# Rotation of q and k on VectorE or GpSimd by plan, bias rows on the sync queue, and a longer DMA latency in the plan

## The chip, the core and the metric

The kernel runs on one core of a Trainium2 chip. A core has five engines that run their own instruction streams in order and wait for one another through semaphores: TensorE (PE, matmuls; PEld is its weight load), VectorE (DVE), ScalarE (ACT), GpSimd (POOL) and SyncE (SP, which here only issues DMA transfers). The metric is device time in microseconds (us) of one execution. The kernel before takes 1269.06 us, the median of three runs (1265.8 to 1271.94).

## The reference

Four decoder layers on x of 256 tokens by 1024, float32. Layers 0 and 3 mix tokens with attention A (a sliding window of 128, 16 query heads on 4 key heads, biases and a learned sink for each head), layer 1 with B (three dilated attentions, merged by their softmax denominators), layer 2 with C (here causal attention in a single block). A mixer is: project to q, k, v; rotate the first 16 of the 64 columns of each head of q and k; attend; project back. After it come a layer norm of alpha\*x + mixer(x), a SwiGLU network of width 2816 and a second layer norm.

```python
def apply_rope(x, cos, sin):
    half = ROT_DIM // 2                       # ROT_DIM = 16, heads of 64
    x1, x2 = x[..., :half], x[..., half:ROT_DIM]
    return concat([x1 * c - x2 * s, x2 * c + x1 * s, x[..., ROT_DIM:]])

def mixer_a(x, w_qkv, b_qkv, sinks, w_o, b_o, cos, sin):
    qkv = x @ w_qkv + b_qkv
    q, k, v = apply_rope(q part), apply_rope(k part), v part
    o, _ = block_attention(q, k, v, 128, 127, True, sinks)
    return o @ w_o + b_o

for i in range(4):
    x = layer_norm(alpha * x + mixer[i % 3](x))
    x = layer_norm(alpha * x + swiglu(x))
```

## The kernel before, in words

**Numbers.** Weights and activations are float32 and are multiplied as two float16 parts each: `whi`, `wlo` of a weight (scaled by 256), `xth`, `xtl` of the transposed input. One product is three matmuls into one PSUM bank (`mm3`, L293 to L295).

**Weights.** They come in chunks of 1024 x 512 (for the last projection of the network also 768 x 512), each chunk in pieces of 128 x 1024. A piece is loaded by a DMA on SP into one of four buffers `raw` (L250), ScalarE makes `whi` of it (L229), VectorE makes `wlo` (L221), and the buffer is then free for the next load. Up to five chunks are alive. The four pieces of the first chunk do not use `raw`: they are loaded at the start, between the four halves of x, into buffers that are not needed yet (L91; their names are htl, oth, otl).

**The plan.** The program of PE, ACT, DVE and POOL is written out in the order that a small planner in the kernel finds while it is built. It keeps a clock `T` for each engine. `do(engine, us, dep, fn)` gives an instruction out if its input is there by the plan, or files it under its due time `dep`; `spend` moves PE's clock on by each matmul and gives out what has become due. A piece of weights is fed when both ACT and DVE would be idle; its first split is due at `T["DMA"] + 2.0`, where `T["DMA"]` is the time at which its buffer came free plus 1.45 (L253 to L257). What the planner believes decides the order alone; at run time each engine goes through its stream in that order and waits where an input is late. SP is not among the engines of the plan: its DMAs stand in an order of their own, given below.

**q and k.** When a chunk of q and k columns has been summed (8 steps over k, for each half t of the tokens), ACT copies the bank to an SBUF tile `qkv` (L864 in mixer A, L924 in B and C), `rope` rotates it in place with four instructions on GpSimd (L408 to L411; the plan gives them 2.2 us), and PE turns it by transposes (L304), after which ACT and DVE split the result (`qkh`, `qkl`). There are 44 such rotations: 12 in the two mixers A (4 of them of half width), 24 in B, 8 in C.

**The start.** `first_chunk` lays out the first chunk of mixer A: dummy matmuls (L1013), transposes of x as its halves land, the first steps over k for both t; then `bias_parts` makes the two float16 parts of mixer A's bias (L1023 on ACT, L1024 on DVE) and copies them to two rows of the tile `abias` by two DMAs that POOL issues (L1020); `angles` and `tables` make the sines and cosines. The bias enters each bank by a matmul with a tile of ones (L300), after the fifth step over k. The raw bias, `araw`, is loaded by the last of four DMAs on POOL (L95).

Of the kernel before, what the change touches and what calls it, by code (L numbers as in the profile page):

```python
# [18 lines left out]
P = 128  # L19
# [24 lines left out]
def trunk(ctx, tc, a, out):  # L44
    nc = tc.nc
    ctx.enter_context(tc.manual_schedule(engines={getattr(mybir.EngineType, e) for e in ("PE", "Activation", "DVE", "Pool")}))
    pool = lambda name, bufs, **kw: ctx.enter_context(tc.tile_pool(name=name, bufs=bufs, **kw))
    RING, RAWS = 5, 4
    const = pool("const", 1)
    raw_p = pool("raw", RAWS)  # L50
    w_p = pool("w", RING)
# [24 lines left out]
    araw = const.tile([P, 2, 20], F32, name="araw")  # L76
# [7 lines left out]
    big0 = big.tile([P, NFB, SEQ], F16, name="htl").rearrange("p f s -> p (f s)").bitcast(F32)  # L84
    stage = [big0[:, :1024], big0[:, 1024:2048]] + [
        big.tile([P, NK, SEQ], F16, name=n).rearrange("p f s -> p (f s)").bitcast(F32) for n in ("oth", "otl")]
    for h in range(2):
        for t in range(NT):
            nc.sync.dma_start(X[t][:, h * 512:h * 512 + 512], a["x"][t * P:(t + 1) * P, h * 512:h * 512 + 512])
            i = 2 * h + t  # L90
            nc.sync.dma_start(stage[i], a["w_a"][0, 0][:, 1024 * i:1024 * i + 1024])  # L91
    nc.gpsimd.dma_start(pos_i, a["positions"].rearrange("(t p) -> p t", p=P))
    nc.gpsimd.dma_start(inv, a["inv"].partition_broadcast(P))
    nc.gpsimd.dma_start(sinks, a["a_sinks"].partition_broadcast(P))
    nc.gpsimd.dma_start(araw, a["a_bias"].rearrange("j (p c) -> p j c", p=P))  # L95

# [5 lines left out]
    T = {"PE": 0.0, "ACT": 0.0, "DVE": 0.0, "POOL": 0.0, "DMA": 0.0}  # L104
# [5 lines left out]
    def do(e, us, dep, fn, then=None, key=None):  # L110

        def give():
            fn()
            T[e] = max(T[e], dep) + us
            if then is not None:
                then(T[e] + HOP)
        if dep <= max(T["PE"], T[e]):
            give()
        else:
            serial[0] += 1  # L120
            due.append((dep, serial[0], give, key))
            due.sort(key=lambda d: d[:2])
# [86 lines left out]
    def new_w(src, n):  # L209
        ring["alive"] += 1  # L210
        assert ring["alive"] <= RING
        hi, lo = (w_p.tile([P, 4096], F16, name=nm) for nm in ("whi", "wlo"))
        return {"hi": hi, "lo": lo, "src": src, "n": n, "ready": [None] * (n // 2), "raw": None, "next": 0,
                "parts": tuple(p.rearrange("p (k n) -> p k n", n=512) for p in (hi, lo))}

    def piece(c, i, r, there, last=None):
        s = slice(1024 * i, 1024 * i + 1024)
        ring["flying"] += 1

        def low(end):  # L220
            do("DVE", dve(1024), end, lambda: nc.vector.scalar_tensor_tensor(  # L221
                c["lo"][:, s], r, WS, c["hi"][:, s], op0=OP.mult, op1=OP.subtract), landed, "w")

        def landed(end):
            c["ready"][i] = end
            ring["flying"] -= 1
            if last is not None:
                last(end)
        do("ACT", act(1024), there, lambda: nc.scalar.activation(c["hi"][:, s], r, AF.Copy, scale=WS), low, "w")  # L229

    def feed_one():

        c = ring["now"]
        if c is None:
            if ring["alive"] == RING:
                return False
            src = next(weights, None)
            if src is None:
                return False
            c = ring["now"] = new_w(*src)  # L240
            loaded.append(c)
        i = c["next"]
        c["next"] += 1
        until(lambda: raws[0] < NEVER)
        T["DMA"] = max(T["DMA"], raws.pop(0)) + 1.45
        raws.append(NEVER)
        slot[0] += 1
        number = slot[0]
        r = raw_p.tile([P, 1024], F32, name="raw")
        nc.sync.dma_start(r, c["src"][:, 1024 * i:1024 * i + 1024])  # L250

        def last(end):

            raws[RAWS - 1 - (slot[0] - number)] = end
        if c["next"] == len(c["ready"]):
            ring["now"] = None
        piece(c, i, r, T["DMA"] + 2.0, last)  # L257
        return True

    slot = [0]  # L260
# [138 lines left out]
    def rope(y, n, t, nh, dep, then):  # L399

        def turn():
            t1 = two.tile([P, 8, ROT], F32, name="rope1")[:, :nh]
            t2 = two.tile([P, 8, ROT], F32, name="rope2")[:, :nh]
            cb = cc[:, t:t + 1, :].to_broadcast([P, nh, ROT])
            sb0 = ss[:, t:t + 1, :h8].to_broadcast([P, nh, h8])
            sb1 = ss[:, t:t + 1, h8:].to_broadcast([P, nh, h8])
            e = nc.gpsimd
            e.tensor_tensor(t1, y[:, :, :ROT], cb, op=OP.mult)  # L408
            e.tensor_tensor(t2[:, :, :h8], y[:, :, h8:ROT], sb0, op=OP.mult)  # L409
            e.tensor_tensor(t2[:, :, h8:], y[:, :, :h8], sb1, op=OP.mult)  # L410
            e.tensor_tensor(y[:, :, :ROT], t1, t2, op=OP.add)  # L411
        do("POOL", 2.2, dep, turn, then)

    def transposed(y, t, n, dst, key):

# [15 lines left out]
    turn = [0]  # L431
# [578 lines left out]
    def spin(n):  # L1010
        ps, b = bank()
        for _ in range(n):
            nc.tensor.matmul(ps, idle[:, :P], idle, start=True, stop=True)  # L1013
        T["PE"] += 0.43 * n
        b["free"] = T["PE"]

    def bias_rows(j, queue):

        for i in range(2):
            queue.dma_start(abias[i:i + 1].rearrange("o (p c) -> o p c", p=P), aparts[:, i, j])  # L1020

    def bias_parts():
        nc.scalar.activation(aparts[:, 0], araw, AF.Copy, scale=WS)  # L1023
        nc.vector.scalar_tensor_tensor(aparts[:, 1], araw, WS, aparts[:, 0], op0=OP.mult, op1=OP.subtract)  # L1024
        bias_rows(0, nc.gpsimd)

    def first_chunk(XT, evac):

        c = new_w(*next(weights))
        c["next"] = 4  # L1030
        land = [3.6, 5.2, 6.0, 7.6, 8.4, 10.0, 10.8, 12.4]
        spin(6)
        wait(land[0])
        transpose_x(0, XT, 0)
        piece(c, 0, stage[0], land[1])
        spin(3)
        wait(land[2])
        transpose_x(1, XT, 0)
        piece(c, 1, stage[1], land[3])
        spin(1)  # L1040
        p = [proj(XT, c, t, evac) for t in range(NT)]
        for f in p[0][:2] + p[1][:2]:
            f()
        T["DMA"] = 12.4
        for t in range(NT):
            wait(land[4 + 2 * t])
            transpose_x(t, XT, 1)
        for f in p[0][2:4] + p[1][2:4]:
            f()
        for i in (2, 3):  # L1050
            piece(c, i, stage[i], land[1 + 2 * i])
        until(lambda: c["ready"][3] is not None)
        bias_parts()
        do("DVE", 2.2, 0.0, angles)
        T["ACT"] += 2.0
        ring["on"] = True
        for f in p[0][4:6] + p[1][4:6]:
            f()
        do("DVE", 1.0, T["ACT"], tables)
        for f in p[0][6:] + p[1][6:]:  # L1060
            f()
        done()
# [3 lines left out]
    for li in range(DEPTH):  # L1066
        kind, j = li % 3, li // 3
# [94 lines left out]
```

## Time and profile before

| | before |
|---|---|
| median of 3 runs | 1269.06 us (1265.8 to 1271.94) |
| the profiled execution | 1272.32 us, of which the span from the first to the last instruction is 1270.5 us |
| busy in the span: PE, DVE, ACT, POOL | 1240.2, 878.8, 668.9, 131.1 us |
| mean granted TensorE clock | 0.993 of 2.4 GHz |

The span is what the trace shows; the 1.8 us around it are the same execution's time outside. The ends of matmuls are modelled, so that PE looks busy between two matmuls that follow each other closely; a wait of PE shows as a start that comes late, with the idle time before it in brackets and the engine or DMA that ended it. Line numbers of this section and of the rows are those of the kernel before; in the changed kernel they are one to two higher.

### The profile page before, as it was taken

The numbers are of one execution on the slowest core, as the hardware profiler recorded it, in microseconds if no ns is written. First come the engines' busy times: TensorE is split into PE (matmuls) and PEld (weight loads), VectorE is DVE, ScalarE is ACT, GpSimd is POOL, SyncE is SP. The second block draws the span as 40 slices with busy tenths as digits, with TensorE's granted clock in tenths as the row PEclk, the third lists the DMA queues.
The fourth block names the chain that finished last, engine by engine and source line by source line (L and its number), as shares of the span: only waits on it lengthen the run. The fifth ranks groups of instructions, "written<-read, shape, count | busy, mean of one in ns | idle before, by whom it ended". The sixth has DMA issues, their size and how long they took to land.

```text
span 1270.5 us, 24604 instructions
## 1 busy us (share of the span) xinstructions
PE 1240.2 (98%) x9990; PEld 828.2 (65%) x9990; DVE 878.8 (69%) x1415; ACT 668.9 (53%) x1102; POOL 131.1 (10%) x270
## 2 busy tenths in 40 slices
PE   7999999999999999999999999999999999999997
PEld 3558888444555555588884445588884455888843
DVE  4798876556676676778665677778665578886632
ACT  4775664336666656546543367546543276465410
POOL 3310000013021203000000122000000132000000
PEclk9999999999999999999999999999999999999999
DMA  6556875546645455357556465457656454676510
GB/s 230 171 166 232 261 253 183 200 149 204 226 135 161 124 180 172 128 166 266 200 183 202 146 218 183 131 165 262 206 183 201 150 164 126 198 258 216 183 51 33
DMA packets 66402, 230.75 MB, mean 182 GB/s; under 512 B 7760, under 2 KB 7792, under 8 KB 66288
## 3 DMA queue, kind: packets, MB, share of 16 engines
q1 hardware_dynamic: 66096, 229.12, 54.5%
q8 instruction: 78, 1.28, 0.4%
q14 instruction: 36, 0.29, 0.1%
q0 software_dynamic: 192, 0.05, 0.0%
HBM read 228.07 MB, written 1.05 MB: 180 GB/s over the span
## 4 chain that ended last, share of the span: by engine, by line
PE 73%; issue 15%; POOL 5%; DVE 4%; ACT 1%; DMA 1%; SPq 0%; POOLq 0%; DVEq 0%; ACTq 0%
PE acc L293 23%; PE acc L294 22%; PE acc L295 22%; PE at L304 3%; POOL qkv L411 2%; POOL rope L408 1%; DVE wlo L221 1%; PE at L544 1%; POOL rope L410 1%; DVE s L521 1%; POOL rope L409 1%; DMA x<-in_x 1%; ACT s L530 0%; DMA raw<-in_w_a 0%; PE pv L295 0%
## 5 line engine op out<-in xcount | busy, mean ns | idle before, releaser
L221 DVE SCALAR_TENSOR_TENSOR wlo<-raw,whi 128x1024 f16<-128x1024 f32 x412 | 495.8, 1229 | 133.6 <-ACT whi L229 129.6
L229 ACT ACTIVATE whi<-raw 128x1024 f16<-128x1024 f32 x412 | 420.6, 1049 | 132.4 <-PE acc L295 54.2
L294 PE MATMUL acc<-xtl,whi 128*128 128x256 f16 (+1 forms) x1664 | 400.6, 256 | 1.1 <-DVE xtl L314 1.1
L295 PE MATMUL acc<-xth,wlo 128*128 128x256 f16 (+1 forms) x1664 | 400.6, 256 | 0.0
L293 PE MATMUL acc<-xth,whi 128*128 128x256 f16 (+1 forms) x1664 | 400.4, 256 | 0.0
L294 PE MATMUL acc<-wlo,xth 128*128 128x512 f16 x480 | 183.6, 382 | 0.8 <-DVE wlo L221 0.6
L293 PE MATMUL acc<-whi,xth 128*128 128x512 f16 x480 | 183.9, 383 | 0.0
L295 PE MATMUL acc<-whi,xtl 128*128 128x512 f16 x480 | 183.5, 382 | 0.0
L295 PEld LDWEIGHTS <-wlo 128*128 128x128 f16 x1664 | 162.8, 98 | 14.7 <-issue 1.5
L294 PEld LDWEIGHTS <-whi 128*128 128x128 f16 x1664 | 162.8, 98 | 13.6
L293 PEld LDWEIGHTS <-whi 128*128 128x128 f16 x1664 | 162.8, 98 | 13.4
L293 PE MATMUL acc<-whi,hth 128*128 128x512 f16 x352 | 133.4, 379 | 0.0
L294 PE MATMUL acc<-wlo,hth 128*128 128x512 f16 x352 | 133.4, 379 | 0.0
L295 PE MATMUL acc<-whi,htl 128*128 128x512 f16 x352 | 133.4, 379 | 0.0
L680 POOL TENSOR_TENSOR mv<-mv,nhalf 128x1 f32<-128x1 f32 x16 | 17.5, 1096 | 829.4 <-DVE mv L677 829.4
L738 ACT ACTIVATE ph<-acc 128x256 f32<-128x256 f32 x88 | 33.4, 379 | 111.2 <-PE acc L295 111.0
L728 DVE SCALAR_TENSOR_TENSOR ph<-ph,acc 128x256 f32<-128x256 f32 x88 | 36.6, 416 | 74.8 <-ACT ph L738 74.8
L295 PEld LDWEIGHTS <-xtl 128*128 128x128 f16 x480 | 47.3, 99 | 59.0 <-issue 3.5
L530 ACT ACTIVATE s<-s,mn 128x257 f32<-128x257 f32 (+5 forms) x128 | 67.1, 526 | 23.7 <-DVE mn L521 22.9
L293 PEld LDWEIGHTS <-xth 128*128 128x128 f16 x480 | 47.2, 98 | 43.1 <-issue 5.1
L294 PEld LDWEIGHTS <-xth 128*128 128x128 f16 x480 | 47.3, 98 | 39.4 <-issue 1.5
L314 DVE TENSOR_TENSOR pl<-at,ph 128x512 f16<-128x512 f32 x76 | 49.5, 658 | 24.9 <-ACT ph L310 24.7
(114 smaller groups left out, 1422.4 us busy)
## 6 DMA issues: line engine op xcount, KB each, us to landing
raw<-in_w_gu SPq DMA_DIRECT2D x176, 512.0 KB, 5.1
raw<-in_w_dn SPq DMA_DIRECT2D x88, 512.0 KB, 4.6
raw<-in_w_b SPq DMA_DIRECT2D x72, 512.0 KB, 4.6
raw<-in_w_c SPq DMA_DIRECT2D x24, 512.0 KB, 5.8
raw<-in_w_a SPq DMA_DIRECT2D x20, 512.0 KB, 5.8
raw<-in_w_ao SPq DMA_DIRECT2D x16, 512.0 KB, 4.8
raw<-in_w_bo SPq DMA_DIRECT2D x8, 512.0 KB, 4.1
raw<-in_w_co SPq DMA_DIRECT2D x8, 512.0 KB, 5.9
```

Source lines behind the costliest of these rows:

```text
L221: do("DVE", dve(1024), end, lambda: nc.vector.scalar_tensor_tensor(c["lo"][:, s], r, WS, c["hi"][:, s], op0=OP.mult, op1=OP.subtract), lan ...
L229: do("ACT", act(1024), there, lambda: nc.scalar.activation(c["hi"][:, s], r, AF.Copy, scale=WS), low, "w")
L293: nc.tensor.matmul(ps, st[0], mv[0], start=start, stop=False)
L294: nc.tensor.matmul(ps, st[0], mv[1], start=False, stop=False)
L295: nc.tensor.matmul(ps, st[1], mv[0], start=False, stop=stop)
L304: nc.tensor.transpose(ps, src, ident)
L314: nc.vector.tensor_tensor(lo, src, hi, op=OP.subtract)
L411: e.tensor_tensor(y[:, :, :ROT], t1, t2, op=OP.add)
L530: do("ACT", act(n) + 0.17, end, lambda: nc.scalar.activation(s[hh][:, pi], s[hh][:, pi], AF.Exp, bias=mine, scale=-1.0, accum_out=q["l"][: ...
L680: nc.gpsimd.tensor_tensor(mv[:, 3:4], mv[:, 2:3], nhalf, op=OP.pow)
L728: nc.vector.scalar_tensor_tensor(th, th, 1.0, g, op0=OP.add, op1=OP.mult)
L738: do("ACT", act(256), T["PE"] + DRAIN, lambda: nc.scalar.activation(th, g, AF.Tanh, scale=0.5 / WS), lambda at: do("DVE", 0.79, at, gate, ...
```

## The change

Three edits. `rope` asks the plan which of VectorE and GpSimd would be through first (0.8 us there, 3.3 us here) and puts the four instructions on that engine. The load of `araw` becomes the first DMA on SP, `bias_parts` stands at the beginning of `first_chunk`, and its two row copies are issued by SP. The plan's due time of a piece of weights is `T["DMA"] + 3.3` in place of `+ 2.0`.

```diff
-    RING, RAWS = 5, 4
+    RING, RAWS, LATE = 5, 4, 3.3
@@
+    nc.sync.dma_start(araw, a["a_bias"].rearrange("j (p c) -> p j c", p=P))
     for h in range(2):
         for t in range(NT):
             nc.sync.dma_start(X[t][:, h * 512:h * 512 + 512], a["x"][t * P:(t + 1) * P, h * 512:h * 512 + 512])
@@
     nc.gpsimd.dma_start(sinks, a["a_sinks"].partition_broadcast(P))
-    nc.gpsimd.dma_start(araw, a["a_bias"].rearrange("j (p c) -> p j c", p=P))
@@
-        piece(c, i, r, T["DMA"] + 2.0, last)
+        piece(c, i, r, T["DMA"] + LATE, last)
@@ def rope
-            e = nc.gpsimd
+            e = nc.vector if quick else nc.gpsimd
             e.tensor_tensor(t1, y[:, :, :ROT], cb, op=OP.mult)
             e.tensor_tensor(t2[:, :, :h8], y[:, :, h8:ROT], sb0, op=OP.mult)
             e.tensor_tensor(t2[:, :, h8:], y[:, :, :h8], sb1, op=OP.mult)
             e.tensor_tensor(y[:, :, :ROT], t1, t2, op=OP.add)
-        do("POOL", 2.2, dep, turn, then)
+
+        quick = max(T["DVE"], dep) + 0.8 <= max(T["POOL"], dep) + 3.3
+        do("DVE" if quick else "POOL", 0.8 if quick else 3.3, dep, turn, then)
@@ def bias_parts
-        bias_rows(0, nc.gpsimd)
+        bias_rows(0, nc.sync)
@@ def first_chunk
         land = [3.6, 5.2, 6.0, 7.6, 8.4, 10.0, 10.8, 12.4]
+        bias_parts()
         spin(6)
@@
         until(lambda: c["ready"][3] is not None)
-        bias_parts()
         do("DVE", 2.2, 0.0, angles)
```

How the streams stand before and after, at three places. All 44 rotations stand on DVE in the changed kernel: POOL's stream shrinks from 204 rows to 20 and DVE's grows from 1190 to 1384.

The head of SP's stream before (x_102 and x_103 are the two halves of the tokens, htl, oth and otl the buffers that hold the first chunk of weights):

```order
L89 DMA x_102<-in_x 128x512
L91 DMA htl<-in_w_a 128x1024
L89 DMA x_103<-in_x 128x512
L91 DMA htl<-in_w_a 128x1024
L89 DMA x_102<-in_x 128x512
L91 DMA oth<-in_w_a 128x1024
L89 DMA x_103<-in_x 128x512
L91 DMA otl<-in_w_a 128x1024
L250 DMA raw<-in_w_a 128x1024 x2
L887 DMA masks<-in_masks 128x1920
L250 DMA raw<-in_w_a 128x1024 x3
```

and now:

```order
L87 DMA araw<-in_a_bias 128x2x20
L90 DMA x_102<-in_x 128x512
L92 DMA htl<-in_w_a 128x1024
L90 DMA x_103<-in_x 128x512
L92 DMA htl<-in_w_a 128x1024
L90 DMA x_102<-in_x 128x512
L92 DMA oth<-in_w_a 128x1024
L90 DMA x_103<-in_x 128x512
L92 DMA otl<-in_w_a 128x1024
L1022 DMA abias<-aparts 1x128x20 x2
L250 DMA raw<-in_w_a 128x1024
L889 DMA masks<-in_masks 128x1920
```

One small load stands ahead of x, and the two bias rows stand behind the first chunk and ahead of every other weight.

ScalarE's stream from the end of the first chunk's splits on, before (sn are the sines, qkv the copies of the first chunk's k columns for the two t, qkh_132 the v columns, qkh_130 the turned k):

```order
L1023 ACTIVATE aparts<-araw 128x40
L1000 ACT_TABLE_LOAD
L1000 ACTIVATE sn<-ang 128x16
L1001 ACTIVATE sn<-ang 128x16
L229 ACTIVATE whi<-raw 128x1024
L864 ACTIVATE qkv<-acc 128x256
L310 ACTIVATE qkh_132<-acc 128x256
L229 ACTIVATE whi<-raw 128x1024
L864 ACTIVATE qkv<-acc 128x256
L229 ACTIVATE whi<-raw 128x1024
L310 ACTIVATE qkh_132<-acc 128x256
L229 ACTIVATE whi<-raw 128x1024 x2
```

and now:

```order
L1002 ACT_TABLE_LOAD
L1002 ACTIVATE sn<-ang 128x16
L1003 ACTIVATE sn<-ang 128x16
L229 ACTIVATE whi<-raw 128x1024
L866 ACTIVATE qkv<-acc 128x256
L310 ACTIVATE qkh_132<-acc 128x256
L866 ACTIVATE qkv<-acc 128x256
L310 ACTIVATE qkh_132<-acc 128x256
L229 ACTIVATE whi<-raw 128x1024
L310 ACTIVATE qkh_130<-at 128x2x128
L229 ACTIVATE whi<-raw 128x1024 x2
```

The second piece of the second chunk stood ahead of the copies of t = 1 and now stands behind them; the bias parts have gone to the head of the stream.

VectorE's stream in mixer C, around the rotation of the second q and k chunk for t = 1, before (s and mn are the masked scores and their row minima, qkl_8549 the low part of the turned q and k of t = 0):

```order
L316 SCALAR_TENSOR_TENSOR htl<-acc,hth 128x512
L221 SCALAR_TENSOR_TENSOR wlo<-raw,whi 128x1024 x6
L314 TENSOR_TENSOR qkl_8549<-at,qkh_8548 128x4x128
L221 SCALAR_TENSOR_TENSOR wlo<-raw,whi 128x1024
L521 ISA s,mn<-at,masks 128x128
```

and now:

```order
L221 SCALAR_TENSOR_TENSOR wlo<-raw,whi 128x1024
L314 TENSOR_TENSOR qkl_8549<-at,qkh_8548 128x4x128
L221 SCALAR_TENSOR_TENSOR wlo<-raw,whi 128x1024
L408 TENSOR_TENSOR rope_8846<-qkv,cc 128x128
L409 TENSOR_TENSOR rope_8847<-qkv,ss 128x8x8
L410 TENSOR_TENSOR rope_8847<-qkv,ss 128x8x8
L411 TENSOR_TENSOR qkv<-rope_8846,rope_8847 128x8x16
L523 ISA s,mn<-at,masks 128x128
```

The rotation stands between the split of a piece of weights and the first scores.

## Rows read from the trace of the kernel before

**Rows 1.** Page, parts 1 and 5: busy us, mean ns, idle time before.

```profile
PE 1240.2 (98%) x9990; PEld 828.2 (65%) x9990; DVE 878.8 (69%) x1415; ACT 668.9 (53%) x1102; POOL 131.1 (10%) x270
...
L221 DVE SCALAR_TENSOR_TENSOR wlo<-raw,whi 128x1024 f16<-128x1024 f32 x412 | 495.8, 1229 | 133.6 <-ACT whi L229 129.6
L229 ACT ACTIVATE whi<-raw 128x1024 f16<-128x1024 f32 x412 | 420.6, 1049 | 132.4 <-PE acc L295 54.2
```

**Rows 2.** Who waited for whom: us in total, times, longest us.

```profile
PE acc L300 <- DMA abias<-aparts: 4.6, 1, 4.6
PE at L304 <- POOL qkv L411: 4.0, 5, 2.1
PE pv L293 <- DVE oy L601: 3.5, 2, 2.7
```

**Rows 3.** Busy time by stretch: span, engines, TensorE clock, DMA share, GB/s.

```profile
20.60:23.90 3.30, 3.30 (x9) 1.18 (x10) 0.68 (x6) 0.00 (x0) 0.00 (x0) 0.53 0.55 160
40.70:44.20 3.50, 3.50 (x10) 1.21 (x9) 1.92 (x2) 1.65 (x3) 0.00 (x0) 0.51 0.79 280
44.50:115.00 70.50, 66.23 (x688) 44.37 (x688) 64.92 (x152) 49.92 (x118) 13.28 (x42) 1.00 0.52 171
295.00:500.00 205.00, 204.40 (x1477) 110.00 (x1475) 141.72 (x216) 127.76 (x200) 42.28 (x84) 1.00 0.54 172
760.90:764.40 3.50, 3.50 (x17) 1.68 (x16) 1.14 (x5) 3.09 (x10) 0.00 (x0) 0.51 0.91 297
1005.00:1085.00 80.00, 76.94 (x590) 44.50 (x588) 65.05 (x151) 50.65 (x122) 22.03 (x58) 0.98 0.43 139
```

**Rows 4.** Timeline of the start: start us, duration us, then idle time before.

```profile
0.74 0.38 SPq L89 DMA_DIRECT2D x<-in_x  x1
...
4.42 0.46 SPq L91 DMA_DIRECT2D otl<-in_w_a  x1
...
15.69 0.56 POOL L1020 DMA_DIRECT2D abias<-aparts  x1 [9.40 <-ACT aparts L1023]
...
20.54 0.59 PE L300 MATMUL acc<-abias,ones 128*128 128x512 f16 x1 [4.64 <-DMA abias<-aparts]
```

**Rows 5.** DMA issues of the first 30 us: KB each, us from issue to landing.

```profile
otl<-in_w_a SPq DMA_DIRECT2D x1, 512.0 KB, 8.5
...
abias<-aparts POOLq DMA_DIRECT2D x2, 5.0 KB, 4.1
```

**Rows 6.** Timeline of the second chunk, mixer A of layer 0.

```profile
27.45 0.39 ACT L864 ACTIVATE qkv<-acc 128x256 f32<-128x256 f32 x1
...
34.10 1.06 ACT L229 ACTIVATE whi<-raw 128x1024 f16<-128x1024 f32 x1 [1.47 <-DMA raw<-in_w_a]
...
35.06 0.58 ACT L864 ACTIVATE qkv<-acc 128x512 f32<-128x512 f32 x1
...
38.34 1.31 POOL L411 TENSOR_TENSOR qkv<-rope,rope 128x128 f32<-128x128 f32 x1
...
39.71 0.66 PE L304 MATMUL at<-ident,qkv 128*128 128x128 f32 x4 [2.10 <-POOL qkv L411]
```

**Rows 7.** Timeline of mixer C, second q and k chunk.

```profile
756.33 0.59 ACT L924 ACTIVATE qkv<-acc 128x512 f32<-128x512 f32 x1
...
756.77 1.21 DVE L221 SCALAR_TENSOR_TENSOR wlo<-raw,whi 128x1024 f16<-128x1024 f32 x1
...
758.12 0.28 DVE L521 CUSTOM_DVE_ANT_0 s<-at,masks 128x128 f32<-128x128 f32 x1
...
758.33 0.28 DVE L521 CUSTOM_DVE_ANT_0 s<-at,masks 128x128 f32<-128x128 f32 x1
...
758.93 1.35 POOL L411 TENSOR_TENSOR qkv<-rope,rope 128x128 f32<-128x128 f32 x1
...
760.33 0.66 PE L304 MATMUL at<-ident,qkv 128*128 128x128 f32 x4 [1.86 <-DVE mn L521]
```

**Rows 8.** Groups by form: busy us, mean ns, idle before.

```profile
L314 DVE TENSOR_TENSOR otl<-at,oth 128x256 f16<-128x256 f32 x32 | 13.3, 418 | 5.6 <-ACT oth L310 5.4
```

## Prediction

> **What bounds the kernel now.** I read the page first: PE is busy for 1240.2 of 1270.5 us, VectorE for 69%, ScalarE for 53%, GpSimd for 10% [rows 1]. So PE is the bound nearly everywhere, and a change that leaves PE's work as it is can win only what PE loses by waiting or by a lower clock. The busy times by stretch say where that is: in mixer B PE is busy for 204.40 of 205 us, so there is nothing to win; in the attention of the two mixers A it is busy for 66.23 of 70.5 and 76.94 of 80 us [rows 3]. The table of waits names the losses: 4.6 us, once, for the bias rows; 4.0 us in five waits for the last instruction of a rotation; 3.5 us in two waits of the product with the values for VectorE [rows 2]. The timelines give each its place, and the stretches with a granted clock of 0.51 to 0.53 [rows 3] show what comes behind a wait: after about 4.6, 2.1 and 1.9 us of idling, PE ran for some 3.4 us at 1.2 GHz before it had 2.4 GHz again.
>
> **The change, part by part** (negative is faster).
>
> *1. The bias rows.* POOL issues the first row copy at 15.69 because it waits 9.40 us for ScalarE's bias parts, which stand behind the first chunk's splits, and PE's bias matmul then starts at 20.54 after 4.64 us of idling [rows 4]; a row copy takes 4.1 us to land [rows 5]. In the new order the parts come first on ACT and DVE, and the two copies follow otl on SP. otl is issued at 4.42 [rows 4] and lands 8.5 us later [rows 5], at 12.9. The copies are behind it and 10 KB long in all; with the half microsecond of item 2 they land at 13.5 to 14.5, and PE wants them at 20.54 - 4.64 + 0.5 = 16.4. The wait goes: -4.6. If the copies were held up, up to all of it would stay, so its bounds are 0 and -4.6. The stretch 20.60 to 23.90 ran at 0.53 with PE always busy [rows 3]; at full clock it takes 0.53 x 3.3 = 1.75 us: -1.5.
>
> *2. A load ahead of x.* SP needs 0.38 to 0.46 us for an issue [rows 4], and everything at the start hangs on x and the first chunk: +0.5 (between 0.4 and, with a slow transfer of its 256 small rows, 1.0). The two bias copies also stand ahead of all `raw` loads, about 1 us of SP's time; those loads queue behind 3 MB that is still on its way until 12.9, which hides it. Without that cover it would be +1.0.
>
> *3. The rotation in the second chunk.* At 34.10 ACT splits a piece of weights for which it had waited 1.47 us; behind it the copy of q comes at 35.06, GpSimd's rotation is through at 39.65, and PE idles 2.10 us [rows 6], followed by 40.70 to 44.20 at 0.51 [rows 3]. With the piece due 1.3 us later in the plan and the four instructions on VectorE the copy is not held up and the rotation takes about 0.7 us in place of the 4 between the copy's end (35.64) and 39.65. -2.1 for the wait, 3.5 x 0.49 = -1.7 for the clock.
>
> *4. What is late next.* With the bias there, PE reaches the second chunk early. Its second piece is now split behind the copies of t = 1: copy 0.39 [rows 6], the v columns' high part of the same shape another 0.39, `whi` 1.05, `wlo` 1.23 [rows 1], with hand-overs about 3.2 us after PE's last matmul of the first chunk. PE has until then two steps over k, six matmuls of 512 columns at 2.4 GHz, 1.3 us, and two transposes, 0.3. A new wait of 3.2 - 1.6, taken as +1.5 (0 to 3.2, the upper end with a stretch at half clock).
>
> *5. The other waits for rotations.* The table has 4.0 us in five waits [rows 2]; without the 2.1 there are 1.9 in four, of which I take -1.5 (0 to -1.9). In mixer C the wait at 760.33 is booked to VectorE, but the rotation's last instruction ends at 758.93 + 1.35 = 760.28: GpSimd it is. The copy ended at 756.92, VectorE is busy with a piece until 757.98 [rows 7], and the new order puts the rotation right behind that piece: done at 758.7, so about 0.45 of the 1.86 us stays: -1.4. Behind it 760.90 to 764.40 ran at 0.51, but with ScalarE busy for 3.09 of 3.50 us [rows 3], so PE would have waited there at any clock: half of 1.7, -0.9 (0 to -1.7).
>
> *6. The price on VectorE.* The trace has no rotation on it. A 256-wide instruction of this kind takes 418 ns [rows 8] and a 128-wide one 0.28 us, with the next starting 0.21 us after it, an accumulator read of 0.08 in between [rows 7]. So a rotation (two 128-wide, two 64-wide) costs at least 4 x 0.11 = 0.45 us by starts and at most 2 x 0.28 + 2 x 0.21 = 0.98 by full durations; I take 0.7, as the fourth instruction needs the others' results. 44 of them are 31 us of VectorE. In mixer B it has 205 - 141.72 = 63 us free for 24 x 0.7 = 17 [rows 3], and a rotation of 0.7 replaces one that lasted 3.4 us in item 5's place and 4 in item 3's, so I cost it at 0 there; the cover is weights split well ahead, and without it all 17 would show. In the attention of the mixers A VectorE is busy for 92% and 81% [rows 3]. Two rotations fall there in each layer, 4 x 0.7 = 2.8, of which I put a third on PE's path: +1.0 (0 to 4 x 0.98 = 3.9).
>
> [...]
>
> *7. The longer latency in the plan* moves splits of weights behind other work on ACT and DVE. Its effect in the second chunk is in item 3. Elsewhere 0: the pieces come chunks ahead, and PE's 204.40 of 205 us covers them. If it made weights late, 1 to 2 us at the start of a layer.
>
> Sum: -4.6 - 1.5 + 0.5 - 2.1 - 1.7 + 1.5 - 1.5 - 1.4 - 0.9 + 1.0 = -10.7. The profiled execution took 1272.3 us, 1270.5 and 1.8 around it; it becomes 1261.6. It was 3.3 us above the median of the runs shown, so on that scale the forecast is 1269.06 - 10.7 = 1258.
>
> **The rivals.**
>
> *A. VectorE gives the start's gain back.* Items 1 to 4 bring layer 0's attention forward by 7.9 us. VectorE has only 70.5 - 64.92 = 5.6 us free in it [rows 3] and gets two rotations (1.4) more, so if its work there cannot shrink, the stretch's end moves by 4.2 and not by 7.9. For it speaks the 92%; against it, that part of this work is weights split ahead for the network, which can be done later. With mixer C's gain of 2.3 lost too, the change is -10.7 + 3.7 + 2.3 = -4.7: 1264.
>
> *B. VectorE becomes the bound: slower.* If mixer B's rotations delay the weights that PE needs next, since a rotation waits at the head of VectorE's stream for ScalarE's copy and the splits queue behind it, then 24 x 0.98 = 23.5 us come on the path: +12.8, 1282. It decides as soon as PE's waits in 295 to 500 us exceed 11 us. Against it: 63 us free, and ScalarE gives the copies out in the same planned order.
>
> *C. The attention waits go as well.* The 3.5 us of waits for VectorE [rows 2] stand where the plan had the order wrong by a little; a new order may not have them, nor a half-speed stretch behind them (1.7): 1258 - 5.2 = 1253. Nothing in the change aims at it, and more work on VectorE speaks against it.
>
> *D. The change does not do what it says:* it does not weigh two engines, all 44 rotations go to one; that is in the sum already.
>
> **How the numbers follow.** Forecast 0.66, A 0.16, B 0.07, C 0.11. The forecast's own range takes items 4, 5 and 6 at their ends: 1252 to 1265. With C's lower side and A's upper one I give 1251 to 1267; B lies outside. A difference of 0.5%, 6.3 us, is about what a measurement of this kernel can tell from none: faster means below 1262.7, and 0.60 of the forecast's 0.66 lies there with all of C, 0.71. Within 0.5%: the rest of the forecast and A, 0.22. Slower: B, 0.07.
>
> **What would show it.** Step by step in the new profile: no wait of PE for abias, and the granted clock at 1.00 behind it; the bias rows landed by 15 us; no wait of transposes for a rotation near 30 us; a short wait for `wlo` in the second chunk's third step; rotations on DVE of 0.45 to 1.0 us each and about 31 us in all; PE busy above 204 us of mixer B's 205; PE waits at the second q and k chunk of mixer C under 1 us. I am wrong if the half-speed stretch comes back near 25 us, if PE waits for weights in mixer B, or if the network of layer 0 does not begin about 7 us earlier than before.

## The result, and the profile after

| | before | changed |
|---|---|---|
| median of 11 runs each, on the same chip | 1271.27 us (1265.8 to 1274.06) | 1263.65 us (1260.64 to 1265.49) |
| ratio | | 0.9939, 95% interval 0.9925 to 0.9954 |
| the profiled execution's span | 1270.5 us | 1261.2 us |
| mean granted TensorE clock in it | 0.993 | 0.996 |

The change makes the kernel 0.6% faster, 7.7 us by the ratio (5.8 to 9.5) and 9.3 us between the two profiled executions. The forecast was -10.7 and rival A -4.7; 7.7 lies half-way between the two.

The page of the changed kernel, parts 1 and 5 (the rows that answer to [rows 1]):

```profile
PE 1235.0 (98%) x9990; PEld 826.4 (66%) x9990; DVE 907.0 (72%) x1591; ACT 668.7 (53%) x1102; POOL 36.4 (3%) x91
...
L221 DVE SCALAR_TENSOR_TENSOR wlo<-raw,whi 128x1024 f16<-128x1024 f32 x412 | 493.4, 1221 | 117.8 <-ACT whi L229 114.3
```

VectorE has 28 us more work and GpSimd 95 us less. PE has the same 9990 instructions and is busy 5.2 us less, for the most part because it runs at half speed for a shorter time (a granted clock of 0.50, where matmuls of 512 columns start 0.43 us apart in place of 0.215; the prediction's 1.2 in place of 2.4 GHz): ahead of the program's last 5 us, one stretch of 6.8 us (70.4 to 77.2) in place of four of 3.4 us.

PE's waits in the changed kernel (us in total, times, longest), as in [rows 2]:

```profile
PE pv L293 <- DVE oy L603: 3.9, 2, 2.6
PE at L304 <- DVE mn L523: 2.0, 3, 0.8
...
PE at L546 <- DVE mn L523: 1.7, 1, 1.7
...
PE at L304 <- DVE qkv L411: 1.4, 2, 1.0
```

The wait for the bias rows is gone, that for the end of a rotation fell from 4.0 to 1.4 us, and those booked to VectorE's row minima (`mn`) are 3.7 us, from 2.4 before, of which 1.9 belonged to a rotation [rows 7]. The start, by timeline (answers to [rows 4]) and, in the second fence, by landings (KB each, us from issue to landing; answers to [rows 5]):

```profile
5.52 1.56 SPq L1022 DMA_DIRECT2D abias<-aparts  x2
...
16.19 0.38 PE L300 MATMUL acc<-abias,ones 128*128 128x512 f16 x1
...
24.27 0.38 PE L294 MATMUL acc<-wlo,xth 128*128 128x512 f16 x1 [0.88 <-DVE wlo L221]
```

```profile
otl<-in_w_a SPq DMA_DIRECT2D x1, 512.0 KB, 9.3
abias<-aparts SPq DMA_DIRECT2D x2, 5.0 KB, 8.6
```

The rows land at about 14.5 us; PE takes them at 16.19 without a wait. What is late next is a `wlo` of the second chunk, for which PE waits 0.88 us. By stretch (span, engines, clock, DMA share, GB/s; answers to [rows 3]):

```profile
41.61:83.42 41.81, 38.41 (x345) 23.29 (x344) 37.29 (x102) 33.37 (x87) 3.58 (x20) 0.92 0.42 134
...
20.60:23.90 3.30, 2.61 (x13) 1.14 (x12) 3.23 (x13) 2.66 (x6) 1.70 (x8) 1.00 0.48 132
295.00:500.00 205.00, 203.99 (x1516) 111.13 (x1515) 156.79 (x307) 130.63 (x210) 0.00 (x0) 1.00 0.53 170
```

The stretch behind the bias rows now runs at 1.00, and mixer B stays full (203.99 of 205 us). The first line is the attention of layer 0, from the fifth to the ninth bias matmul. The same of before:

```profile
49.37:87.33 37.96, 35.60 (x342) 21.82 (x340) 34.85 (x91) 32.58 (x85) 7.69 (x29) 1.00 0.39 124
```

It became 3.85 us longer, so about half of what the start won is lost there. (Some of the 3.85 is order: in the changed kernel four transposes of the attention stand ahead of the ninth bias matmul that stand behind it before. Counted on to the first matmul of the network, with the same work of PE on both sides, the stretch takes 55.98 us in place of 52.54, 3.4 more.)

The table follows the gain through the program: when PE starts an instruction, in us relative to before, in the profiled executions of this and of six kernels of the next section. Each column is one execution. The last two have the same order on every engine up to 270 us and differ by up to 1.0 us before that, so a difference of 1 us between two columns can be chance.

| PE starts (before, us) | changed | bias alone | rotation alone | latency alone | bias + rotation | bias + latency | the same, rotation on VectorE from layer 1 on |
|---|---|---|---|---|---|---|---|
| 2nd bias matmul (23.47) | -5.77 | -6.11 | 0.28 | -0.66 | -5.84 | -6.22 | -6.11 |
| 3rd, second chunk (30.81) | -4.60 | -4.54 | 2.34 | 0.33 | -3.95 | -5.33 | -5.21 |
| 5th, attention (49.37) | -7.76 | -7.89 | -0.58 | -4.23 | -5.81 | -10.23 | -9.36 |
| 9th, its end (87.33) | -3.91 | -7.50 | 2.83 | -0.98 | -3.18 | -7.80 | -6.84 |
| layer 0's network, second half (219.16) | -6.49 | -7.19 | 4.46 | -3.56 | -3.17 | -10.37 | -9.41 |
| layer 1's network, behind B (546.47) | -7.65 | -7.19 | 3.52 | -3.84 | -4.34 | -10.64 | -10.27 |
| layer 2's network, behind C (832.59) | -9.00 | -8.08 | 1.64 | -7.08 | -6.46 | -13.65 | -10.91 |
| end (1270.5) | -9.33 | -7.06 | 2.19 | -7.09 | -5.03 | -13.65 | -10.37 |

### The profile page after: what moved, and what is told of

The parts are those of the page before. It is cut to its first block, busy times and chain, and to the rows that moved or that the text cites. A ratio compares the mean times of both kernels' runs of the same rounds, so it can differ in the third digit from the quotient of the medians.

```text
span 1261.2 us, 24537 instructions
## 1 busy us (share of the span) xinstructions
PE 1235.0 (98%) x9990; PEld 826.4 (66%) x9990; DVE 907.0 (72%) x1591; ACT 668.7 (53%) x1102; POOL 36.4 (3%) x91
## 4 chain that ended last, share of the span: by engine, by line
PE 88%; DVE 5%; ACT 2%; issue 2%; DMA 2%; SPq 0%; POOL 0%; POOLq 0%; DVEq 0%; ACTq 0%
PE acc L293 27%; PE acc L294 27%; PE acc L295 27%; PE at L304 5%; PE at L546 2%; DVE wlo L221 2%; ACT s L532 1%; DVE s L523 1%; ACT whi L229 1%; DMA x<-in_x 1%; PE pv L293 1%; DMA raw<-in_w_a 1%; PE pv L295 1%; PE pv L294 1%; DMA raw<-in_w_co 0%
## 5 line engine op out<-in xcount | busy, mean ns | idle before, releaser
L221 DVE SCALAR_TENSOR_TENSOR wlo<-raw,whi 128x1024 f16<-128x1024 f32 x412 | 493.4, 1221 | 117.8 <-ACT whi L229 114.3
L310 ACT ACTIVATE hth<-pl 128x256 f16<-128x256 f32 x88 | 36.2, 412 | 60.1 <-DVE pl L731 60.1
L655 DVE SCALAR_TENSOR_TENSOR x<-x,acc 128x512 f32<-128x512 f32 x32 | 21.3, 684 | 56.6 <-PE acc L295 56.6
```

The lines of the kernel that those rows point to most:

```text
L310: nc.scalar.activation(hi, src, AF.Copy, scale=1.0 if scale is None else scale)
L655: nc.vector.scalar_tensor_tensor(y[:, s], y[:, s], ALPHA * WS, ps, op0=OP.mult, op1=OP.add)
```

## The experiments

**The three edits alone.** Theory: the prediction's items. Rival: the gains belong to other edits than those the prediction credits. Each kernel is the changed one with two edits taken back.

*The bias edit alone.*

```diff
-        piece(c, i, r, T["DMA"] + LATE, last)
+        piece(c, i, r, T["DMA"] + 2.0, last)
-            e = nc.vector if quick else nc.gpsimd
+            e = nc.gpsimd
-        do("DVE" if quick else "POOL", 0.8 if quick else 3.3, dep, turn, then)
+        do("POOL", 2.2, dep, turn, then)
```

> The kernel before with the bias edit alone (raw bias first on the sync queue, its parts and row copies at the front). Sum of the prediction's items 1 and 2: -4.6 - 1.5 + 0.5 = -5.6 us, less up to 1.5 for the new wait of item 4: ratio to before 0.9956 to 0.9968, and the network of layer 0 begins 4 to 6 us earlier. Rival A (VectorE, full in layer 0's attention, gives back whatever is won ahead of it, with or without rotations on it): the second chunk ends 4 us or more earlier but the network of layer 0 begins only 1 to 3 us earlier, ratio 0.998 to 0.999.

Ratio 0.9953 (0.9938 to 0.9969), -6.0 us. Items 1 and 2 have their size: -6.1 at the second bias matmul, for -5.6. The total comes near it by chance, since the kernel then loses 1.6 us up to the third bias matmul (item 4) and wins 3.4 up to the fifth, where the stall of item 3 is gone without item 3's edit. Layer 0's attention gives only 0.4 us of it back, and its network begins 7.2 us earlier, more than the 4 to 6 expected: an early start alone doesn't run into VectorE.

*The rotation edit alone.*

```diff
-        piece(c, i, r, T["DMA"] + LATE, last)
+        piece(c, i, r, T["DMA"] + 2.0, last)
-    nc.sync.dma_start(araw, a["a_bias"].rearrange("j (p c) -> p j c", p=P))
+    nc.gpsimd.dma_start(araw, a["a_bias"].rearrange("j (p c) -> p j c", p=P))
-        bias_rows(0, nc.sync)
+        bias_rows(0, nc.gpsimd)
```

(`bias_parts()` stands again behind the first chunk.)

> The kernel before with the rotations put on VectorE by plan, alone. Items 3, 5 and 6: -2.1 - 1.7 - 1.5 - 1.4 - 0.9 + 1.0 = -6.6 us if item 3 needs nothing but the faster rotation; -2.8 if the wait in the second chunk stays because ScalarE's copy is still held up by a piece that has not landed: ratio 0.9948 to 0.9978. The bias wait of 4.6 us stays. Rival B (rotations at the head of VectorE's stream delay weights): ratio 1.000 or more, and PE waits in mixer B.

Ratio 1.0029 (1.0017 to 1.004): slower, where I had a gain. The table has the place: +4.5 by layer 0's network, -0.9 in mixer B, -1.9 in C; rival B has the ratio, but not the place. Of the 4.5, an estimated 1.6 are clock, from the lengths of the half-speed stretches. Behind the same wait for the bias rows as in before (4.62 us), PE ran at half speed for 4.7 us in this execution and not for 3.2 (span, engines, clock):

```profile
19.00:25.80 6.80, 4.99 (x13) 1.87 (x14) 1.72 (x6) 0.82 (x1) 0.00 (x0) 0.52 0.53 175
```

The other executions of this kernel had mean clocks of 0.990 to 0.997 and took 1271.5 to 1275.9 us. The one at 0.997 took 1272.5, more than the median of the kernel before (1270.2, most at 0.994 to 0.995), so the loss isn't clock alone.

*The latency alone.*

```diff
-    nc.sync.dma_start(araw, a["a_bias"].rearrange("j (p c) -> p j c", p=P))
+    nc.gpsimd.dma_start(araw, a["a_bias"].rearrange("j (p c) -> p j c", p=P))
-            e = nc.vector if quick else nc.gpsimd
+            e = nc.gpsimd
-        do("DVE" if quick else "POOL", 0.8 if quick else 3.3, dep, turn, then)
+        do("POOL", 2.2, dep, turn, then)
```

> The kernel before with the longer DMA latency in the plan alone. My theory: it only matters where item 3's copy is held up, and there GpSimd is still slow: 0 to -1 us, ratio 0.999 to 1.000. Rival: the order was wrong by the latency in many places, and the whole of item 3's 3.8 us hangs on it: ratio 0.997.

Ratio 0.9959 (0.9942 to 0.9975), -5.2 us, where I had 0 for all but item 3's stall. The timeline of mixer C, second q and k chunk, with the rotation on GpSimd as in [rows 7]; first the split ahead of the copy in the kernel before, then this kernel:

```profile
753.94 1.06 ACT L229 ACTIVATE whi<-raw 128x1024 f16<-128x1024 f32 x1 [2.02 <-DMA raw<-in_w_co]
```

```profile
750.14 1.06 ACT L229 ACTIVATE whi<-raw 128x1024 f16<-128x1024 f32 x1 [0.39 <-DMA raw<-in_w_co]
...
751.18 0.60 ACT L924 ACTIVATE qkv<-acc 128x512 f32<-128x512 f32 x1
...
753.40 1.35 POOL L411 TENSOR_TENSOR qkv<-rope,rope 128x128 f32<-128x128 f32 x1
...
754.80 0.66 PE L304 MATMUL at<-ident,qkv 128*128 128x128 f32 x4 [0.39 <-POOL qkv L411]
```

ScalarE waits 0.39 us for the piece of weights in place of 2.02, and the copy is at 751.18, against 756.33 in [rows 7] (3.8 of these 5.2 us had been won before mixer C). The rotation takes as long as ever (its last instruction 1.35 us), and PE's 1.86 us of waiting are 0.39. The wait was booked to the rotation, but what made it was a split of weights that stood ahead of the copy on ScalarE before its data had landed.

*Bias and rotation, without the latency.*

```diff
-        piece(c, i, r, T["DMA"] + LATE, last)
+        piece(c, i, r, T["DMA"] + 2.0, last)
```

> The changed kernel without the longer DMA latency in the plan (bias edit and rotations on VectorE). If the latency does nothing the ratio is that of the changed kernel, 0.994; if the copy of item 3 is held up again, 3 to 4 us of it are lost: 0.9965. If the give-back in layer 0's attention (the trace of the changed kernel has 8.0 us won at the bias matmuls of the third chunk and 3.9 at those of the projection) is one of order and not of VectorE's load, it is not there, and the ratio is 0.991.

Ratio 0.9988 (0.9977 to 0.9999), worse than all three outcomes that I had named: the rotation takes 4.4 us of the bias edit's 6 away, and the latency is worth 0.5% in the changed kernel. The trace shows the second outcome's hold-up: in the second chunk ScalarE waits 4.5 us for a piece of weights ahead of the copy, and PE then 2.2 us for the rotation.

**The version that follows from it: bias and latency, rotation on GpSimd.**

```diff
-        quick = max(T["DVE"], dep) + 0.8 <= max(T["POOL"], dep) + 3.3
-        do("DVE" if quick else "POOL", 0.8 if quick else 3.3, dep, turn, then)
+        quick = False
+        do("DVE" if quick else "POOL", 2.2, dep, turn, then)
```

> The changed kernel with the 44 rotations back on GpSimd at their old price of 2.2 in the plan; the bias edit and the latency of 3.3 stay. Theory (the gains are the bias edit's and the latency's, and the rotation on VectorE costs in layer 0): the ratios of the edits alone add up, 0.9953 and 0.9959 make 0.991, about 1259 us, some 4 us under the changed kernel; no half-speed stretch near 20 or 40 us. Rival (with the bias early, the second chunk is too tight for GpSimd's rotation, as the prediction's item 3 has it, so that VectorE earns its cost only in company of the other two edits): PE waits 2 us or more for the rotation in the second chunk, a half-speed stretch stands behind it, and the ratio is 0.994 or more.

1259.06 us, ratio 0.9908 (0.9891 to 0.9925), span 1256.9: faster than the kernel before and, by the two ratios, 3.9 us faster than the changed one (4.6 by the medians, beside which the kernel before took 1270.3 and 1271.3; the intervals of the ratios touch at 0.9925). The edits add up (0.9953 x 0.9959 = 0.9912); the rival is out. PE doesn't wait for the second chunk's second rotation, and no half-speed stretch stands before 69 us.

**Where the rotation on VectorE costs.**

```diff
-        quick = max(T["DVE"], dep) + 0.8 <= max(T["POOL"], dep) + 3.3
-        do("DVE" if quick else "POOL", 0.8 if quick else 3.3, dep, turn, then)
+        quick = layer[0] > 0
+        do("DVE" if quick else "POOL", 0.8 if quick else 2.2, dep, turn, then)
```

(`layer[0]` is set to `li` at the head of each layer.)

> The changed kernel with layer 0's rotations on GpSimd (price 2.2) and those of layers 1 to 3 on VectorE. Theory (the rotation on VectorE costs in layer 0's first mixer alone, 4.5 us, and gains 0.9 in mixer B and 1.9 in mixer C, as the run with that edit alone had it): 1 to 3 us below the kernel with all rotations on GpSimd, ratio 0.989 to 0.991. Rival (mixer C's gain is the one that the latency has already, so the two do not add): the same as with all on GpSimd within 1 us. Second rival (the cost is that of VectorE everywhere): 2 us or more above it.

1260.93 us, ratio 0.9922 (0.9906 to 0.9939), 1.9 us above the last kernel (1260.2 to 1261.9, against 1258.0 to 1261.0 there): nearer to the second rival. By the table mixer B gains 0.6 us more than there, which can be chance, but C gains 0.6 in place of 3.0. The timeline of C says why:

```profile
744.39 1.06 ACT L229 ACTIVATE whi<-raw 128x1024 f16<-128x1024 f32 x1 [1.73 <-DMA raw<-in_w_co]
...
745.48 1.23 DVE L221 SCALAR_TENSOR_TENSOR wlo<-raw,whi 128x1024 f16<-128x1024 f32 x1 [1.91 <-ACT whi L229]
746.62 0.28 DVE L408 TENSOR_TENSOR rope<-qkv,cc 128x128 f32<-128x128 f32 x1
...
747.65 0.63 PE L304 MATMUL at<-ident,qkv 128*128 128x128 f32 x4 [1.19 <-DVE qkv L411]
747.75 0.40 ACT L532 ACTIVATE s<-s,mn 128x128 f32<-128x128 f32 x1 [1.81 <-DVE mn L523]
```

One late load holds up ScalarE, then VectorE's `wlo`, then the rotation behind it, and the row minima behind that: PE waits 1.19 us and ScalarE 1.81. On GpSimd the rotation needs the copy alone and runs beside the `wlo`: with the latency alone its first instruction starts at 751.85, 0.07 us behind the end of the copy, beside a `wlo` from 751.23 to 752.46 (and takes 0.91 us).

**Is 3.3 the right latency, or a lucky one?** Two other values in the kernel with bias and latency:

```diff
-    RING, RAWS, LATE = 5, 4, 3.3
+    RING, RAWS, LATE = 5, 4, 4.6
```

> As the kernel with rotations on GpSimd, bias early and latency, but with 4.6 us of latency in place of 3.3. Theory (the gain is that pieces are planned no earlier than they land; the issues of the weight pieces in the kernel before land a median 5.1 us after their issue, and the plan with 3.3 counts on 4.75): nearly all is had at 3.3, the time is within 1.5 us of that with 3.3, and ScalarE's waits for DMA in the mixers are no longer. Rival (the gain is luck of the order that the plan falls into): the time moves by 3 us or more in either direction, with waits of PE at new places.

1262.49 us, ratio 0.9936 (0.9918 to 0.9954): 3.4 us above 3.3, with new PE waits in layer 0's attention (2.16 us for a `wlo`, until 59.05). The rival is right in layer 0; mixer C, though, gains 3.8 us, as the theory has it.

```diff
-    RING, RAWS, LATE = 5, 4, 3.3
+    RING, RAWS, LATE = 5, 4, 2.65
```

> As the kernel with rotations on GpSimd, bias early and latency, but with 2.65 us, half-way between the 2.0 of before and 3.3. Theory (pieces planned no earlier than they land): the time lies between that of the bias edit alone (ratio 0.9953) and that with 3.3, about 0.993. Rival (luck of the order): it lies outside of the two, by 2 us or more.

1266.58 us, ratio 0.9963 (0.9948 to 0.9979): the theory's 0.993 is out. It is worse than with 3.3 by 7 us and not told apart from 2.0 (0.9953, 0.9938 to 0.9969), so the rival's 2 us beyond both neighbours is not shown. Its nine runs spread from 1262.1 to 1267.7, and the profiled one is the slowest. In that one layer 0 keeps only 1.7 us of the start's gain; C gains 3.1. The timeline of layer 0's second chunk:

```profile
31.39 1.06 ACT L229 ACTIVATE whi<-raw 128x1024 f16<-128x1024 f32 x1 [3.16 <-DMA raw<-in_w_a]
32.35 0.58 ACT L866 ACTIVATE qkv<-acc 128x512 f32<-128x512 f32 x1
...
33.91 2.48 DVE L221 SCALAR_TENSOR_TENSOR wlo<-raw,whi 128x1024 f16<-128x1024 f32 x2 [0.21 <-ACT whi L229]
33.98 1.33 POOL L409 TENSOR_TENSOR rope<-qkv,ss 128x64 f32<-128x64 f32 x1
35.28 1.29 POOL L410 TENSOR_TENSOR rope<-qkv,ss 128x64 f32<-128x64 f32 x1
36.65 0.45 POOL L411 TENSOR_TENSOR qkv<-rope,rope 128x128 f32<-128x128 f32 x1
37.16 1.11 PE L304 MATMUL at<-ident,qkv 128*128 128x128 f32 x4 [3.95 <-POOL qkv L411]
```

Here 2.65 was not long enough: ScalarE stood 3.16 us ahead of the copy. The loads of the first 40 us land much later than any plan so far believes (7.1 to 7.3 us after issue for three of the second chunk; the plan has 1.45 + 2.65 from the free buffer). The same three took 5.9 to 6.1 us in the profiled execution with 3.3, so part of this is a slow execution. The loads of mixer A's weights issued from 7 to 40 us (KB each, median us from issue to landing), in this kernel:

```profile
raw<-in_w_a SPq DMA_DIRECT2D x8, 512.0 KB, 7.4
```

**The stretch that gives back.** The kernel with bias and latency, with the old latency for the pieces of layer 0's attention:

```diff
-        piece(c, i, r, T["DMA"] + LATE, last)
+        piece(c, i, r, T["DMA"] + (2.0 if 11 <= number <= 24 else LATE), last)
```

> The kernel with rotations on GpSimd, bias early and latency 3.3, but with the old 2.0 for the pieces 11 to 24 of the queue, those that are split during layer 0's attention. With 3.3 for all, that attention gave back 3.3 us of what the start had won (landmark before it -11.06 us, behind it -7.80); with 2.0 for all it gave back 0.4. Theory (the longer latency puts splits on VectorE right in front of row maxima for which PE waits, and this is the whole give-back): about 2.9 us less, ratio 0.9885, 1256 us, PE's waits between 60 and 75 us under 2.5 us in all and no half-speed stretch there. Rival (the give-back comes from the early arrival: VectorE has no room in that stretch whatever the order): the same ratio as with 3.3 for all, 0.991. Second rival (an order that neither kernel had, with waits of its own): 3 us or more above that.

1262.44 us, ratio 0.9924 (0.9901 to 0.9947): 2 us worse by the ratio and 3.4 by the median, and not better. The attention still gives back 2.1 us (2.4 with 3.3 for all; fifth to ninth bias matmul), now without a half-speed stretch, so neither the latency of these pieces nor the clock is the cause. The ratio is the rival's, but an early arrival alone isn't the cause either: bias alone arrives 7.9 us early and loses 0.4, the latency alone 4.2 early and loses 3.3. What the losing kernels share is a twelfth split in that stretch (table below); why the planner puts it there with 2.0 for these pieces stays open. Lost with it is a gain of 2.2 us between the start of layer 0's network and its second half, which every kernel with 3.3 in that stretch has. The trace shows what is lost: a split stands in the middle of layer 0's first norm, as in the kernel before:

```profile
109.99 1.22 DVE L221 SCALAR_TENSOR_TENSOR wlo<-raw,whi 128x1024 f16<-128x1024 f32 x1
...
111.91 0.75 DVE L688 SCALAR_TENSOR_TENSOR x<-x,mv,qkl 128x512 f32<-128x512 f32 x1
...
112.81 0.63 PE L304 MATMUL at<-ident,x 128*128 128x128 f32 x4 [1.29 <-DVE x L688]
```

PE waits 1.29 us here and 0.51 for the `xtl` behind it; with 2.0 for pieces 11 to 24 it waits 1.12 and 0.51, again behind a `wlo` between the norm's two halves. With 3.3 for all no `wlo` stands there, and PE waits for neither.

```diff
-        piece(c, i, r, T["DMA"] + LATE, last)
+        piece(c, i, r, T["DMA"] + (2.0 if number <= 60 else LATE), last)
```

> The same kernel, but with the old 2.0 for the first 60 pieces (all of layer 0's first mixer and the start of its network) and 3.3 for the rest. Theory (in mixer C the longer latency pays in its own right, 3 us, whatever the start is): until then the landmarks of the run with the bias edit alone, -7.2 to -8.1 us, and 2.3 to 3 us more behind mixer C; ratio 0.9953 - 0.0022 = 0.993, 1261 us, and no PE wait of over 1.1 us at the second q and k chunk of mixer C. Rival (that gain hangs on the order that the start leaves behind): 0.995.

1262.05 us, ratio 0.9923 (0.9902 to 0.9943), as the theory had it: -7.42 at layer 1's network, -10.40 behind mixer C, PE's wait at the second chunk there 0.66 us. The gain in C is the latency's own: 2.6 to 3.8 us in all six kernels that have 2.65 or more there and the rotation on GpSimd, 0.9 with the bias edit alone.

What layer 0's attention takes in all twelve kernels (from the fifth bias matmul to the ninth, and on to the network's first matmul; counted in the traces):

| | to the ninth, us | to the network, us | VectorE busy up to the ninth, us | `wlo` splits | rotations on VectorE | at half speed, us |
|---|---|---|---|---|---|---|
| before; latency of 2.65; latency from piece 61 on | 37.96; 37.96; 37.95 | 52.54; 52.54; 52.53 | 34.85; 34.86; 34.87 | 11 | 0 | 0 |
| bias alone | 38.35 | 53.23 | 34.62 | 11 | 0 | 3.4 |
| bias + latency with 2.0 for its pieces | 40.10 | 54.26 | 36.83 | 12 | 0 | 0 |
| bias + latency; the same, rotation on VectorE from layer 1 on | 40.38; 40.48 | 54.55; 54.65 | 36.70; 36.71 | 12 | 0 | 3.4 |
| latency alone | 41.21 | 55.38 | 36.76 | 12 | 0 | 6.8 |
| latency of 4.6 | 43.55 | 57.69 | 37.29 | 12 | 0 | 0 |
| bias + rotation | 40.59 | 55.17 | 37.63 | 12 | 2 | 0 |
| rotation alone; changed | 41.37; 41.81 | 55.95; 55.98 | 37.74; 37.29 | 12 | 2 | 6.8 |

VectorE is free for some 3 us at the least, and, but for the kernel with 4.6, the length by and large follows the work on it. Compared at the same time at half speed, and counted on to the network, one split more costs 1.7 us (54.26 against 52.53), two rotations 0.9 (55.17 against 54.26) or 0.6 (55.98 against 55.38). Two pairs with the same order of PE there show what half speed costs: 0.7 us for a stretch of 3.4 (53.23 against 52.54), 0.8 for one of 6.8 (55.95 against 55.17). These are single executions, and the orders differ otherwise, so the sizes are estimates. The twelfth split comes with the longer latency as well as with the rotation on VectorE. The row of the kernel with bias and latency (span, engines, clock), to compare with the two of the last section:

```profile
39.14:79.52 40.38, 37.21 (x345) 22.82 (x344) 36.70 (x95) 34.34 (x87) 7.40 (x29) 0.96 0.47 155
```

## Why the prediction was partly right

The time fell within the range and on the side forecast; that the sum came out near is luck, two errors that cancel: layer 0's attention lost 3.85 us where item 6 had an estimated 0.5 for it, and 2.6 us were won right behind it where item 7 had nothing. One of the prediction's own signs of being wrong came true: the network of layer 0 begins 4.3 us earlier (101.91 to 97.59), not about 7. And one bound does not come out of the sum: items 4, 5 and 6 at their ends give about 1254 to 1265, not 1252; nothing hangs on it. Item by item, in the changed kernel's row of the table:

- *Items 1 and 2* (-5.6): -5.77 at the second bias matmul, -6.11 with the edit alone. Right. The rows land 8.6 us after their issue, behind `otl`, within the time that the prediction gave them.
- *Item 4* (+1.5): +1.17 up to the third bias matmul, of which 0.88 are PE's wait for the second piece's `wlo` at 24.27. Right.
- *Item 3* (-3.8): -3.2 up to the attention. The size is right, the reason wrong. The stall vanished with each edit alone: from the third to the fifth bias matmul the bias edit wins 3.4 us, the rotation 2.9, the latency 4.6. It needed a particular order to exist. With bias and latency in, VectorE does worse than GpSimd there (-3.2 against -4.2 to -4.9 in the three kernels that have the rotation on GpSimd and the same order up to there). In the changed kernel's second chunk:

```profile
33.68 1.06 ACT L229 ACTIVATE whi<-raw 128x1024 f16<-128x1024 f32 x1 [1.19 <-DMA raw<-in_w_a]
34.65 0.58 ACT L866 ACTIVATE qkv<-acc 128x512 f32<-128x512 f32 x1
34.77 1.23 DVE L221 SCALAR_TENSOR_TENSOR wlo<-raw,whi 128x1024 f16<-128x1024 f32 x1 [0.97 <-ACT whi L229]
...
35.91 0.28 DVE L408 TENSOR_TENSOR rope<-qkv,cc 128x128 f32<-128x128 f32 x1
36.11 0.22 DVE L409 TENSOR_TENSOR rope<-qkv,ss 128x64 f32<-128x64 f32 x1
36.25 0.22 DVE L410 TENSOR_TENSOR rope<-qkv,ss 128x64 f32<-128x64 f32 x1
36.50 0.29 DVE L411 TENSOR_TENSOR qkv<-rope,rope 128x128 f32<-128x128 f32 x1
...
37.14 1.28 ACT L532 ACT_TABLE_LOAD   x1 [0.97 <-DVE mn L523]
...
37.75 0.63 PE L304 MATMUL at<-ident,qkv 128*128 128x128 f32 x4 [0.56 <-DVE mn L523]
```

  The copy is done at 35.23, but VectorE is in a `wlo` until about 35.9. The rotation, 0.88 us from 35.91 to 36.79, pushes the row minima back, for which ScalarE waits 0.97 us. I had costed the rotation as if VectorE were free when the copy ends.
- *Item 5* (-3.8): -1.2 in mixer B and -1.4 in C. In C this was the latency's to win, 3.0; the rotation on VectorE loses 1.7 of it.
- *Item 6* (+1.0): the failed step, though not by the rotation's price. Layer 0's attention takes 3.85 us more, 3.4 counted on to the network. The two rotations there cost an estimated 0.6 to 0.9, a little over the 0.5 that a third of their 1.4 makes; in layer 3's attention they show no cost (38.37 us, before 38.96). What the prediction put at nothing is the order: the new plan puts a twelfth split into that stretch, 1.7 us, and PE's longer waits there are followed by a half-speed stretch, some 0.8 us. A rotation takes 0.88 us, between the bounds but a quarter over the 0.7 taken: in the rows above its instructions start 0.20, 0.14 and 0.25 us apart, and the last takes 0.29.
- *Item 7* (0): also failed. The latency alone is worth 5.2 us: in the changed kernel it shows as 2.2 us won where layer 0's network begins (the split that no longer stands in the norm) and, less what VectorE loses, as item 5's gain in C.

*Rival A* named the place and nearly the size (the end of the attention moves by 4.2; it moved by 3.9), but not the cause: bias alone loses 0.4 there, so that an early start does not suffice. Of mixer C's gain of 2.3, which it gave up, 1.4 came. *B* and *C* fell: PE is busy for 203.99 of 205 us in mixer B, and the waits of the attention grew (3.5 to 3.9 us for `oy`, and those for `mn`). *D*: 44 rotations went to VectorE, as the sum had it.

## What to carry to other kernels

A wait booked to an instruction can belong to what held up the streams before it: follow it back to the first instruction that waited for data (here ScalarE's split, 2.02 us for a DMA, ahead of the copy in mixer C) before pricing a faster version of the last link. An elementwise step on an idle engine that is slow can be worth more than a quick one on an engine whose stream has late loads in it: here 0.9908 with the rotation on GpSimd (2.1 us on average in the kernel before) against 0.9939 with it on VectorE (0.88 us). And a plan's constant that moves the order has no slope: 2.0, 2.65, 3.3 and 4.6 us gave 0.9953, 0.9963, 0.9908 and 0.9936; 3.3 stands apart, the others are not all told apart. The part that holds at several values (mixer C's 3 us) carries over; the rest is one order against another. A comparison of a stage's length needs kernels with the same time at half speed in it, and landmarks with the same work before them: the cost of two rotations was 1.4 us by the first two kernels at hand (41.81 against 40.38), and 0.6 to 0.9 so compared.

## What the runs showed of the hardware

GpSimd's rotation is slow when VectorE splits weights beside it. Of its 176 instructions in the kernel before, 101 meet no `wlo`, and none of these takes over 0.79 us; all 29 that take over 0.9 us, up to 1.38, have a `wlo` beside them that started 0.02 to 0.57 us earlier, and they end 0.11 to 0.32 us after it does (the 23 of 128x128 0.31 to 0.32). The kernel with 2.65 shows two in a row (above): 128x64 instructions of 1.33 and 1.29 us beside two `wlo`, where the same form takes 0.32 us in the median in the kernel before (1.01 + 1.33 + 1.29 + 0.45 make a rotation of 4 us). The `wlo` pays as well: its mean is 1229 ns with the rotations on GpSimd and 1221 without. Of the 63 beside a rotation 13, which started behind a GpSimd instruction that was still running, take 1.33 to 1.48 us and end 1.08 to 1.09 us after it does; none without a rotation takes over 1.25. In the kernel before, a rotation takes 1.1 to 3.9 us, 2.1 on average.

The same wait does not bring the same half-speed stretch: around the end of 4.6 us of idling for the bias rows PE's clock was at half speed for 3.4 us in the kernel before (0.2 of them still in the wait; 0.53 granted from 20.54 to 23.90) and for 6.8 us in that with the rotation alone (2.1 of them in the wait; 0.52 from 19.00 to 25.80).
